# The mLSTM gates' vector steps spread among the input projections, and two output-gate stores issued by ScalarE, in a hybrid encoder layer

## The chip, the cores and the metric

The kernel runs on one core of one Trainium2 chip. The core has five engines with a queue of their own: TensorE (PE in the profile; its weight loads are PEld), VectorE (DVE), ScalarE (ACT), GpSimd (POOL) and SyncE (SP), which here only issues DMA transfers. The engines run side by side and wait for each other through semaphores; each engine takes its own instructions in the order in which they were written to its queue. The metric is the device time of one execution, in microseconds (us).

## The reference

One encoder layer for 2048 tokens of width 1024. A normalised and modulated input goes through one combined projection whose columns feed two groups of heads: windowed attention, and a bidirectional chunkwise mLSTM with 4 heads of 128. Both are normalised, joined, projected and added; then comes a SwiGLU feed-forward part.

```python
proj = hmix @ w_in
q_a, k_a, v_a, q_m, k_m, v_m, o_m, gates = jnp.split(proj, IN_SPLITS, axis=-1)
att = banded_attention(q_a, k_a, v_a, sink)
qk = jax.nn.silu(centred_dwconv(jnp.concatenate([q_m, k_m], axis=-1), conv_w, conv_b))
i_f, f_f, i_b, f_b = jnp.split(gates + b_gates, 4, axis=-1)
h_fwd = mlstm_chunkwise(qm, km, vm, i_f, f_f)
h_bwd = flip(mlstm_chunkwise(flip(qm), flip(km), flip(vm), flip(i_b), flip(f_b)))
h_m = sigmoid(o_m) * rms_norm(h_fwd + h_bwd)
x = x + gate1 * (jnp.concatenate([att, h_m], axis=-1) @ w_out)
```

What the change touches is, first, the gates of the mLSTM. Per direction, head and chunk of 128 tokens:

```python
logf = blocks(jax.nn.log_sigmoid(f_pre))
bcum = jnp.cumsum(logf, axis=-1)
a = b_last[..., None] - bcum + ig
w = jnp.exp(a - jnp.max(a, axis=-1)[..., None])
m_new = jnp.maximum(bl + m_st, am)            # over the chunks, in order
decay = jnp.exp(bl + m_st - m_new)
m_t = jnp.maximum(bcum + m_prev, running maximum)
inter = jnp.exp(g - m_t)
```

There are 2 directions x 4 heads x 16 chunks = 128 rows of 128 tokens, so that all gates fit in one 128 x 128 tile. Second, it touches the store of the output gate o_m (a tanh of it, kept in DRAM until the heads are joined).

## The kernel before

**Stages.** Tokens are handled in NB = 4 blocks of 512 and NT = 16 chunks of 128. The core normalises and transposes the input (hT), multiplies the natural-order columns (values and gate pre-activations, gn), then runs the transposed projections with the convolution (`conv_tile`), the mLSTM, attention with further projections in between, the output projection, and the feed-forward part.

**A projection.** `proj_mm` (L497) writes 24 matmuls of 128x512 for one block (8 parts of the contraction, each with three products of split operands) into a PSUM buffer gps, of which there are two; so the third block can begin only when the first block's buffer has been read for the last time. `conv_tile` does the four blocks of one head's q or k. When a block's matmuls are written, ACT evicts it with the middle tap (cacc, L524) and two edge columns (L525); DVE later reads the same PSUM buffer twice for the other two taps (`sides`, L511 and L512), which frees it. ACT then takes a tanh (ctanh), DVE one more step on it (L121, from the helper `beat`), and SP stores the block (qk_d).

**The order.** In this part the order of DVE, ACT, POOL and SP is the order of the program text (`manual_schedule`), and PE's is that of the matmuls in the text too. A loop of 252 steps sets it: at step i it first lets the generators whose due step has come write their next piece, and then `pull(1)` writes one projection matmul and counts down the list `soon`, in which `sides` and the rest were put with a distance in steps:

```python
for i in range(2 * 96 + 60):
    for j, g in enumerate(steps):
        while due[j] <= i:
            due[j] = next(g)
    ...
    pull(1)
```

So a number of a step fixes only the place in each queue: a DVE instruction written at step 52 runs as soon as DVE has done those ahead of it and its inputs are there, and not when PE comes to its 52nd matmul. For a matmul of the gates it is the place among the projection matmuls.

**The generators.** `steps` holds `gates()` and `w_out_ops()`. The second prepares the output projection's weights: SP loads pieces (bx, by), POOL multiplies and subtracts them (L949, L951, four times L962), SP stores them (wo_d). `gates()` is the gate computation. Its text yields the step at which the next piece is due: 2, 52, 60, 68, 92. Its pieces are, in order: the two PE transposes of gn; reductions of the identity that make selection tiles (pick, spot, rowm); the copies out of PSUM, log-sigmoid (Exp, Ln, reciprocal), two scans for the cumulative sum b, r = ig - b, two scans for the running maximum cm, and the last column of each chunk (st); a small matmul rps that turns st by head; a scan over chunks (mn) and its shifted forms (rw); Exp; rx and two small matmuls cps that spread them again; the row values (mc, ux, it, em, wr); four stores to bc_d and three PE transposes into rT, wT and eT.

**Attention.** Outside the stretches ordered by hand a scheduler orders the engines' instructions. Within attention, units of 128 queries x 4 heads go through `score` (PE L780/L781, DVE L784, ACT L786), `normalize` (POOL L800), `transpose` (PE L807; ACT L140 and DVE L141 split the result into apth and aptl) and `values` (PE L819/L820), and `pull` sets projection matmuls between. `o_tiles` makes the output gates: ACT takes a tanh (oth, L569, one buffer), and SP stores it to og_d (L570). There are 16 such stores: four of head 0, written before attention begins, and then those of head 1 and of heads 2 and 3.

Of the kernel before, what the change touches and what calls it, by code (L numbers as in the profile page):

```python
# [17 lines left out]
MUL, ADD, SUB, MAX, MIN = ALU.mult, ALU.add, ALU.subtract, ALU.max, ALU.min  # L18
# [7 lines left out]
NT = T // P  # L26
# [10 lines left out]
def hybrid_layer_kernel(  # L37
# [5 lines left out]
    pe, dve, act, pool, sp = nc.tensor, nc.vector, nc.scalar, nc.gpsimd, nc.sync  # L43
    x, out = x[0], out[0]
# [513 lines left out]
    def o_tiles(heads, blocks, ws_):  # L558

        if not ws_:  # L560
            ws_.extend(proj_cols(C_OM + h * P) for h in heads)
        for n in blocks:
            for h, w in zip(heads, ws_):
                ps = bank("g", "gps")
                yield from proj_mm(ps, w, n)
                pl, tag = oslots[0]
                oslots.rotate(-1)
                t = pl.tile([P, 512], F32, tag=tag, name="oth", bufs=1)
                act.activation(t, ps, AF.Tanh, scale=0.5)  # L569
                sp.dma_start(og_d[n, :, :, h], t.rearrange("p (c t) -> p c t", c=4))  # L570
# [265 lines left out]
    def gates():  # L836
# [9 lines left out]
        dve.tensor_reduce(out=pick, in_=ident.rearrange("p (q c) -> p q c", c=NT), axis=mybir.AxisListType.X, op=ADD)  # L846
        for sl, o in ((lo_, spot[lo_]), (hi_, spot[hi_, ::-1])):
            dve.tensor_reduce(out=o, in_=ident[sl].rearrange("p (q c) -> p c q", c=NT), axis=mybir.AxisListType.X, op=ADD)
        dve.tensor_copy(rowm, ident[:8, :8].unsqueeze(2).to_broadcast([8, 8, NT]))
# [9 lines left out]
        dve.memset(rw, 0.0)  # L859
        act.activation(e, e, AF.Exp)  # L860
        dve.tensor_scalar(u, e, 1.0, None, ADD)
        act.activation(l, u, AF.Ln)
        dve.scalar_tensor_tensor(t2, u, -1.0, e, ADD, SUB)
        dve.reciprocal(u, u)
        dve.tensor_tensor(t2, t2, u, MUL)
# [3 lines left out]
        dve.tensor_tensor_scan(b[hi_, ::-1], ones[hi_, ::-1], l[hi_, ::-1], 0.0, MUL, ADD)  # L869
        dve.tensor_tensor(r, ig, b, SUB)  # L870
# [6 lines left out]
        yield 52  # L877
# [9 lines left out]
        yield 60  # L887
        act.activation(rw[:, 2], rw[:, 2], AF.Exp)
        yield 68
# [13 lines left out]
        dve.tensor_scalar(ux, cm, mc[:, 0:1], None, MAX)  # L903
        act.activation(it, ux, AF.Exp, bias=mc[:, 0:1], scale=-1.0)
        act.activation(wr, r, AF.Exp, bias=mc[:, 1:2])
        dve.tensor_tensor(em, b, ux, ADD)
        act.activation(em, em, AF.Exp, scale=-1.0)
        dve.tensor_scalar(it, it, float(128 ** -0.5), None, MUL)
        dve.tensor_scalar(ux, ux, -1.0, None, MUL)
        yield 92  # L910
# [1090 lines left out]
```

## Time and profile before

| | |
|---|---|
| median of three runs | 2270.06 us (2265.61 to 2271.12) |
| profiled execution, its own time | 2264.91 us |
| its span | 2263.1 us |
| mean granted clock of TensorE | 0.994 |
| PE busy | 2218.3 us, 98% |
| DVE busy | 1603.8 us, 71% |
| ACT busy | 1060.8 us, 47% |
| POOL busy | 1041.1 us, 46% |
| chain that ended last | PE 88%, DVE 6%, ACT 3%, DMA 2% |

The profile is of one execution. A row of a timeline gives the start in us from the span's beginning, the duration, engine, line, operation, what is written from what, shapes and count; in brackets stands how long the engine idled before it and which instruction's end released it. Several alike are joined in one row (x3). A row of the stretches gives for each engine the busy time, the number of instructions and then PEclk, the clock that TensorE was granted as a share of full speed, the DMA share and GB/s. Idle time of an engine other than the one that sets the pace costs nothing by itself.

### The profile page before, as it was taken

The page shows a single profiled execution, that of the slowest core. Times are in us where ns is not written, and L with a number is a line of the kernel's source. Part 1 is how long each engine was busy: PE and PEld are TensorE (multiplying, and loading weights), DVE is VectorE, ACT ScalarE, POOL GpSimd, SP SyncE. Part 2 cuts the span into 40 slices and gives each one's busy share as a digit, 9 for nine tenths or more (in the row PEclk, how much of TensorE's full clock was granted, in tenths as well). Part 3 has the DMA queues.
Part 4 walks back from the last instruction along what each step waited for, and adds up shares of the span by engine and source line. Part 5 has one row for each costly group of instructions (what it writes and reads, how often), then busy time and mean ns, then how long its engine had stood idle before and what let it go on. Part 6 is the DMA issues. An engine that isn't in the chain of part 4 may idle for free.

```text
span 2263.1 us, 32366 instructions
## 1 busy us (share of the span) xinstructions
PE 2218.3 (98%) x10818; PEld 1858.4 (82%) x10818; DVE 1603.8 (71%) x2942; ACT 1060.8 (47%) x2209; POOL 1041.1 (46%) x904
## 2 busy tenths in 40 slices
PE   6998999999999999999999999999999999999998
PEld 4997888888788878888888888888888888888887
DVE  6775677656688887886667777777767665785694
ACT  5433666544578846354445444433333333233452
POOL 1015635334343333436666664467666664692020
PEclk9999999999999999999999999999999999999999
DMA  8565755685666575764343454534333374543462
GB/s 328 166 204 181 239 170 170 188 241 171 201 188 186 174 248 205 266 236 152 107 147 112 158 181 166 174 126 140 98 112 98 112 259 140 172 149 94 146 216 93
DMA packets 337064, 391.28 MB, mean 173 GB/s; under 512 B 20875, under 2 KB 234235, under 8 KB 336897
## 3 DMA queue, kind: packets, MB, share of 16 engines
q1 hardware_dynamic: 336672, 389.17, 52.7%
q8 instruction: 85, 1.39, 0.3%
q14 instruction: 83, 0.67, 0.1%
q10 hardware_dynamic: 224, 0.04, 0.0%
HBM read 269.95 MB, written 119.19 MB: 172 GB/s over the span
## 4 chain that ended last, share of the span: by engine, by line
PE 88%; DVE 6%; ACT 3%; DMA 2%; issue 1%; POOL 0%; SPq 0%; ACTq 0%; POOLq 0%; DVEq 0%
PE gps L497 14%; PE fp L56 12%; PE fp L57 12%; PE fp L58 12%; PE fo L58 5%; PE fo L57 5%; PE fo L56 5%; PE ops L56 2%; PE ops L58 2%; PE ops L57 2%; PE kvp L621 1%; PE num L708 1%; PE atp L807 1%; PE num L710 1%; PE pv L56 1%
## 5 line engine op out<-in xcount | busy, mean ns | idle before, releaser
L497 PE MATMUL gps<-hT,whi 128*128 128x512 f32 x1088 | 396.5, 419 | 6.8 <-DVE cacc L512 6.8
L58 PE MATMUL fo<-w,al 128*128 128x512 f32 x616 | 239.8, 389 | 0.2 <-DVE al L1755 0.2
L57 PE MATMUL fo<-w,ah 128*128 128x512 f32 x616 | 239.7, 389 | 0.0
L56 PE MATMUL fo<-w,ah 128*128 128x512 f32 x616 | 239.7, 389 | 0.0
L497 PE MATMUL gps<-hT,wlo 128*128 128x512 f32 x544 | 226.6, 417 | 0.0
L497 PEld LDWEIGHTS gps<-hT,whi 128*128 128x128 f32 x1088 | 200.2, 190 | 31.0 <-ACT cacc L528 7.2
L56 PE MATMUL fp<-T,S 128*128 128x512 f32 x528 | 206.7, 391 | 0.1
L57 PE MATMUL fp<-T,S 128*128 128x512 f32 x528 | 205.6, 389 | 0.0
L58 PE MATMUL fp<-T,S 128*128 128x512 f32 x528 | 205.4, 389 | 0.0
L1755 DVE TENSOR_TENSOR al<-al,ah 128x1024 fp32r<-128x1024 f32 x77 | 115.9, 1509 | 106.2 <-ACT ah L1754 106.2
L1754 ACT ACTIVATE ah<-al 128x1024 fp32r<-128x1024 f32 x77 | 81.6, 1060 | 180.4 <-DMA al<-a_d 178.7
L1457 DVE TENSOR_TENSOR S<-sf,S 128x512 fp32r<-128x512 f32 x86 | 127.7, 1523 | 36.8 <-ACT S L1456 36.8
L1457 DVE TENSOR_TENSOR A<-graw,A 128x512 fp32r<-128x512 f32 x86 | 126.4, 1488 | 19.2 <-ACT A L1456 18.9
L58 PE MATMUL fp<-B,A 128*128 128x512 f32 x352 | 136.9, 389 | 0.0
L56 PE MATMUL fp<-B,A 128*128 128x512 f32 x352 | 136.9, 389 | 0.0
L57 PE MATMUL fp<-B,A 128*128 128x512 f32 x352 | 136.9, 389 | 0.0
L58 PEld LDWEIGHTS fo<-w,al 128*128 128x128 f32 x616 | 115.6, 188 | 24.6 <-DVE al L1755 0.6
L56 PEld LDWEIGHTS fo<-w,ah 128*128 128x128 f32 x616 | 115.6, 188 | 24.3
L57 PEld LDWEIGHTS fo<-w,ah 128*128 128x128 f32 x616 | 115.6, 188 | 24.0
L800 POOL TENSOR_SCALAR ap<-ap,adn 128x384 f32<-128x384 f32 (+1 forms) x124 | 70.6, 589 | 133.1 <-PE atp L807 62.0
L1461 POOL TENSOR_TENSOR sf<-A,A22r 128x512 f32<-128x512 f32 x42 | 58.4, 1391 | 150.8 <-DMA A22r<-in_w_ffn_in_dram 133.9
L1624 DVE SCALAR_TENSOR_TENSOR g<-t,g 128x512 f32<-128x512 f32 x44 | 40.9, 929 | 117.6 <-ACT t L1623 117.6
(440 smaller groups left out, 6146.6 us busy)
## 6 DMA issues: line engine op xcount, KB each, us to landing
al<-a_d SPq DMA_DIRECT2D x77, 512.0 KB, 4.2
wmod<-in_w_mod_dram SPq DMA_DIRECT2D x48, 512.0 KB, 7.5
graw<-in_w_ffn_in_dram SPq DMA_DIRECT2D x43, 512.0 KB, 3.9
a_d<-ka SPq DMA_DIRECT2D x66, 256.0 KB, 5.0
bc<-bc_d SPq DMA_DIRECT2D x64, 256.0 KB, 4.4
hop_d<-n SPq DMA_DIRECT2D x56, 256.0 KB, 3.8
a_d<-u SPq DMA_DIRECT2D x55, 256.0 KB, 4.7
mqk<-qk_d SPq DMA_DIRECT2D x44, 256.0 KB, 4.4
```

The source lines that it names most:

```text
L56: pe.matmul(o, lh, rh, start=first, stop=False, skip_group_check=skip)
L57: pe.matmul(o, lh, rl, start=False, stop=False, skip_group_check=skip)
L58: pe.matmul(o, ll, rh, start=False, stop=last, skip_group_check=skip)
L497: pe.matmul(ps, w[i == 2][:, k, :], hT[n](i == 1, k), start=(k == 0 and i == 0), stop=(k == KT - 1 and i == 2))
L621: pe.matmul(kvp[:, :129], kn, vw, start=True, stop=True)
L708: pe.matmul(num[:, d, :129], sc[:, d, :], va_c, start=True, stop=st is None)
L800: pool.tensor_scalar(p, p, dn[:, g:g + 1], 0.0, MUL, ADD)
L1457: dve.tensor_tensor(t[:, 1, :], f, t[:, 0, :].bitcast(F32), SUB)
L1461: add.tensor_tensor(f1, a21, a22, ADD)
L1624: dve.scalar_tensor_tensor(g0, t0, 1.0, g0, ADD, MUL)
L1754: act.activation(ah, al.bitcast(F32), AF.Copy)
L1755: dve.tensor_tensor(al, al.bitcast(F32), ah.bitcast(F32), SUB)
```

## The change

Two edits.

The gate computation keeps its instructions, but its text yields more often: the steps are now 2, 7, 11, 14, 28, 36, 52, 62, 76, 84, 92, 100 and 112. The reductions to pick, spot and rowm move from the front to behind the two scans that make b. The matmul rps moves from step 52 to 62, the matmuls cps from 68 to 84, the stores to bc_d and the final transposes from 92 to 112.

And of the four output-gate stores of head 1, the first two are issued by ACT's queue instead of SP's.

```diff
--- before.py
+++ after.py
@@ -567,7 +567,7 @@
                 oslots.rotate(-1)
                 t = pl.tile([P, 512], F32, tag=tag, name="oth", bufs=1)
                 act.activation(t, ps, AF.Tanh, scale=0.5)
-                sp.dma_start(og_d[n, :, :, h], t.rearrange("p (c t) -> p c t", c=4))
+                (act if heads == (1,) and n < 2 else sp).dma_start(og_d[n, :, :, h], t.rearrange("p (c t) -> p c t", c=4))
 
     later = []
 
@@ -843,10 +843,6 @@
         pick = s2.tile([P, 8], F32, name="pick", bufs=1)
         spot = s2.tile([P, NT], F32, name="spot", bufs=1)
         rowm = s2.tile([8, 8, NT], F32, name="rowm", bufs=1)
-        dve.tensor_reduce(out=pick, in_=ident.rearrange("p (q c) -> p q c", c=NT), axis=mybir.AxisListType.X, op=ADD)
-        for sl, o in ((lo_, spot[lo_]), (hi_, spot[hi_, ::-1])):
-            dve.tensor_reduce(out=o, in_=ident[sl].rearrange("p (q c) -> p c q", c=NT), axis=mybir.AxisListType.X, op=ADD)
-        dve.tensor_copy(rowm, ident[:8, :8].unsqueeze(2).to_broadcast([8, 8, NT]))
         yield 2
         ig, fg = gt("ig"), gt("fg")
         act.activation(fg, ps[:, P:2 * P], AF.Copy)
@@ -857,16 +853,26 @@
         dve.memset(zr, 0.0)
         rw = s2.tile([8, 3, NT], F32, name="rw", bufs=1)
         dve.memset(rw, 0.0)
+        yield 7
         act.activation(e, e, AF.Exp)
+        yield 11
         dve.tensor_scalar(u, e, 1.0, None, ADD)
+        yield 14
         act.activation(l, u, AF.Ln)
         dve.scalar_tensor_tensor(t2, u, -1.0, e, ADD, SUB)
         dve.reciprocal(u, u)
+        yield 28
         dve.tensor_tensor(t2, t2, u, MUL)
         dve.tensor_tensor(l, t2, l, SUB)
         dve.scalar_tensor_tensor(l, fg, 0.0, l, MIN, ADD)
         dve.tensor_tensor_scan(b[lo_], ones[lo_], l[lo_], 0.0, MUL, ADD)
         dve.tensor_tensor_scan(b[hi_, ::-1], ones[hi_, ::-1], l[hi_, ::-1], 0.0, MUL, ADD)
+        yield 36
+        dve.tensor_reduce(out=pick, in_=ident.rearrange("p (q c) -> p q c", c=NT), axis=mybir.AxisListType.X, op=ADD)
+        for sl, o in ((lo_, spot[lo_]), (hi_, spot[hi_, ::-1])):
+            dve.tensor_reduce(out=o, in_=ident[sl].rearrange("p (q c) -> p c q", c=NT), axis=mybir.AxisListType.X, op=ADD)
+        dve.tensor_copy(rowm, ident[:8, :8].unsqueeze(2).to_broadcast([8, 8, NT]))
+        yield 52
         dve.tensor_tensor(r, ig, b, SUB)
         dve.tensor_tensor_scan(cm[lo_], zr[lo_], r[lo_], -3e38, ADD, MAX)
         dve.tensor_tensor_scan(cm[hi_, ::-1], zr[hi_, ::-1], r[hi_, ::-1], -3e38, ADD, MAX)
@@ -874,7 +880,7 @@
         for sl, j in ((lo_, 127), (hi_, 0)):
             dve.tensor_scalar(st[sl, 0], spot[sl], b[sl, j:j + 1], None, MUL)
             dve.scalar_tensor_tensor(st[sl, 1], spot[sl], cm[sl, j:j + 1], st[sl, 0], MUL, ADD)
-        yield 52
+        yield 62
         ps = bank("c", "rps")
         pe.matmul(ps[:8, :2 * NT], pick, st.rearrange("p j c -> p (j c)"), start=True, stop=True)
         sr = s2.tile([8, 2, NT], F32, name="sr", bufs=1)
@@ -884,9 +890,9 @@
         dve.tensor_copy(rw[:, 0, 1:], mn[:, :-1])
         dve.tensor_tensor(rw[:, 1], sr[:, 0], mn, SUB)
         dve.tensor_tensor(rw[:, 2], rw[:, 1], rw[:, 0], ADD)
-        yield 60
+        yield 76
         act.activation(rw[:, 2], rw[:, 2], AF.Exp)
-        yield 68
+        yield 84
         rx = s2.tile([8, 8, NT], F32, name="rx", bufs=1)
         dve.tensor_tensor(rx, rowm, rw[:, 2].unsqueeze(1).to_broadcast([8, 8, NT]), MUL)
         ps = bank("c", "cps")
@@ -901,13 +907,15 @@
         act.activation(q4(dec[:, 64:])[:, :, ::-1], q4(ps[:, P + 64:2 * P]), AF.Copy)
         ux, it, em, wr = gt("gux"), gt("git"), gt("gem"), gt("gwr")
         dve.tensor_scalar(ux, cm, mc[:, 0:1], None, MAX)
+        yield 92
         act.activation(it, ux, AF.Exp, bias=mc[:, 0:1], scale=-1.0)
         act.activation(wr, r, AF.Exp, bias=mc[:, 1:2])
         dve.tensor_tensor(em, b, ux, ADD)
+        yield 100
         act.activation(em, em, AF.Exp, scale=-1.0)
         dve.tensor_scalar(it, it, float(128 ** -0.5), None, MUL)
         dve.tensor_scalar(ux, ux, -1.0, None, MUL)
-        yield 92
+        yield 112
         for d, sl in ((0, lo_), (1, hi_)):
             sp.dma_start(bc_d[:, :, d, :].rearrange("h c t -> (h c) t"), ux[sl])
             sp.dma_start(bc_d[:, :, 2 + d, :].rearrange("h c t -> (h c) t"), it[sl])
```

How the instructions stand. VectorE, at the two scans for b (which the order names SCALAR_TENSOR_TENSOR on L868 and L869 and the profile TENSOR_TENSOR_SCAN); "gates" is the tile of all gate values. Before:

```order
L868 SCALAR_TENSOR_TENSOR gates<-ones_r,gates 64x128
L869 SCALAR_TENSOR_TENSOR gates<-ones_r,gates 64x128
L870 TENSOR_TENSOR gates<-gates 128x128
L871 SCALAR_TENSOR_TENSOR gates<-gates 64x128
L872 SCALAR_TENSOR_TENSOR gates<-gates 64x128
L875 TENSOR_SCALAR st<-spot,gates 64x16
L876 SCALAR_TENSOR_TENSOR st<-spot,gates,st 64x16
L875 TENSOR_SCALAR st<-spot,gates 64x16
L876 SCALAR_TENSOR_TENSOR st<-spot,gates,st 64x16
L511 SCALAR_TENSOR_TENSOR cacc<-gps,cvw,cacc 128x511
L512 SCALAR_TENSOR_TENSOR cacc<-gps,cvw,cacc 128x511
L881 COPY sr<-rps 8x32
```

The same place in the changed kernel (the lines of the new text):

```order
L868 SCALAR_TENSOR_TENSOR gates<-ones_r,gates 64x128
L869 SCALAR_TENSOR_TENSOR gates<-ones_r,gates 64x128
L511 SCALAR_TENSOR_TENSOR cacc<-gps,cvw,cacc 128x511
L512 SCALAR_TENSOR_TENSOR cacc<-gps,cvw,cacc 128x511
L871 TENSOR_REDUCE pick<-ident 128x8
L873 TENSOR_REDUCE spot<-ident 64x16 x2
L874 COPY rowm<-ident 8x128
L876 TENSOR_TENSOR gates<-gates 128x128
L877 SCALAR_TENSOR_TENSOR gates<-gates 64x128
L878 SCALAR_TENSOR_TENSOR gates<-gates 64x128
L881 TENSOR_SCALAR st<-spot,gates 64x16
L882 SCALAR_TENSOR_TENSOR st<-spot,gates,st 64x16
```

L511 and L512 of the first block now stand right behind the scans for b; the reductions and the steps from r to st follow them.

TensorE, at rps, one piece of the difference (gps is the projection's PSUM buffer):

```order
 L497 MATMUL gps<-hT_767,wlo 128x512
 L497 MATMUL gps<-hT_767,whi 128x512
-L879 MATMUL rps<-st,pick 8x32
 L497 MATMUL gps<-hT_771,whi 128x512
 L497 MATMUL gps<-hT_767,wlo 128x512
```

It stands ten projection matmuls further on. In the same way cps goes 16 matmuls further on and the transposes 20.

VectorE, from st to rx, before which PE's cps can't run. Before:

```order
L881 COPY sr<-rps 8x32
L883 SCALAR_TENSOR_TENSOR mn<-sr 8x16
L884 COPY rw<-mn 8x15
L885 TENSOR_TENSOR rw<-sr,mn 8x16
L886 TENSOR_TENSOR rw<-rw 8x16
L511 SCALAR_TENSOR_TENSOR cacc<-gps,cvw,cacc 128x511
L512 SCALAR_TENSOR_TENSOR cacc<-gps,cvw,cacc 128x511
L121 SCALAR_TENSOR_TENSOR cacc<-ctanh,cacc 128x512
L891 TENSOR_TENSOR rx<-rowm,rw 8x128
```

Now:

```order
L511 SCALAR_TENSOR_TENSOR cacc<-gps,cvw,cacc 128x511
L512 SCALAR_TENSOR_TENSOR cacc<-gps,cvw,cacc 128x511
L121 SCALAR_TENSOR_TENSOR cacc<-ctanh,cacc 128x512
L887 COPY sr<-rps 8x32
L889 SCALAR_TENSOR_TENSOR mn<-sr 8x16
L890 COPY rw<-mn 8x15
L891 TENSOR_TENSOR rw<-sr,mn 8x16
L892 TENSOR_TENSOR rw<-rw 8x16
L511 SCALAR_TENSOR_TENSOR cacc<-gps,cvw,cacc 128x511
L512 SCALAR_TENSOR_TENSOR cacc<-gps,cvw,cacc 128x511
L897 TENSOR_TENSOR rx<-rowm,rw 8x128
```

The convolution's steps of one more block (L511, L512 of block 1 and L121 of block 0) stand ahead of sr, and those of block 2 ahead of rx.

ScalarE, at the first of the two moved stores, one piece of the difference:

```order
 L569 ACTIVATE oth<-gps 128x512
 L792 ACTIVATE adn<-adn 128x4
-L140 ACTIVATE apth<-atp 128x512 x3
+L140 ACTIVATE apth<-atp 128x512
+L570 DMA og_d<-oth 512x1x128
+L140 ACTIVATE apth<-atp 128x512 x2
 L786 ACTIVATE ap,ars<-ap,nmx 128x256 x3
```

The store stands behind the first of three apth copies; the second store follows its tanh directly. In VectorE's queue the scheduler sets one L784 of the next unit ahead of the second and third aptl at this place. All else in attention and behind it stands as before.

## The prediction

> **What bounds the kernel now.** I read the page's first lines and its costliest groups, then the waits of PE, PE's timeline with the granted clock by stretch and the chain of waits around the longest wait, and at last the timelines of DVE, ACT and POOL there.
>
> ```profile
> span 2263.1 us, 32366 instructions
> PE 2218.3 (98%) x10818; PEld 1858.4 (82%) x10818; DVE 1603.8 (71%) x2942; ACT 1060.8 (47%) x2209; POOL 1041.1 (46%) x904
> L497 PE MATMUL gps<-hT,whi 128*128 128x512 f32 x1088 | 396.5, 419 | 6.8 <-DVE cacc L512 6.8
> ```
>
> PE is busy for 98% of the span: what an edit is worth is what it takes from, or adds to, PE's idle time and cold clock. The projections' matmuls (L497) wait for 6.8 us in all, in one piece, on DVE's L512. Timeline of PE, one piece of the chain of waits (matmuls at full pace), and stretches (busy time of PE, PEld, DVE, ACT and POOL, then PEclk):
>
> ```profile
> 192.69 1.19 PE L497 MATMUL gps<-hT,whi 128*128 128x512 f32 x2 [6.83 <-DVE cacc L512]
> 194.66 0.28 PE L879 MATMUL rps<-st,pick 128*8 128x32 f32 x2
> ...
> 199.81 0.46 PE L894 MATMUL cps<-rx,ones_r 8*128 8x128 f32 x2
> 200.20 0.50 PE L497 MATMUL gps<-hT,wlo 128*128 128x512 f32 x1
> ...
> 206.27 36.31 PE gps L497 x160
> ...
> 185.90:192.60 6.70, 0.00 (x0) 0.00 (x0) 6.46 (x8) 1.50 (x4) 6.54 (x9) 0.80 0.55 181
> 192.70:196.70 4.00, 4.00 (x10) 2.71 (x11) 1.62 (x5) 1.83 (x2) 4.00 (x5) 0.50 0.00 0
> ```
>
> PE stops at 185.86 (192.69 less 6.83), when block 2 of the first tile wants the PSUM buffer of block 0. After it the clock is 0.50 for 4.0 us, which costs 2.0 us more. So 8.8 us is all that the gate part can give back. At full pace a matmul takes 36.31/160 = 0.227 us.
>
> Why L512 is late (DVE, then POOL, then one row of ACT):
>
> ```profile
> 176.70 0.28 DVE L846 TENSOR_REDUCE pick<-ident 128x8 f32<-128x128 f32 x1
> ...
> 177.79 0.27 DVE L855 SCALAR_TENSOR_TENSOR gates<-gates 128x128 f32<-128x128 f32 x1
> ...
> 182.03 1.55 DVE L868 TENSOR_TENSOR_SCAN gates<-ones_r,gates 64x128 f32<-64x128 f32 x1
> 183.59 1.36 DVE L869 TENSOR_TENSOR_SCAN gates<-ones_r,gates 64x128 f32<-64x128 f32 x1
> 184.99 0.65 DVE L870 TENSOR_TENSOR gates<-gates 128x128 f32<-128x128 f32 x1
> 185.67 0.83 DVE L871 TENSOR_TENSOR_SCAN gates<-gates 64x128 f32<-64x128 f32 x1
> ...
> 187.88 1.19 DVE L876 SCALAR_TENSOR_TENSOR st<-spot,gates,st 64x16 f32<-64x16 f32 x1
> 189.08 1.21 DVE L875 TENSOR_SCALAR st<-spot,gates 64x16 f32<-64x16 f32 x1
> 190.33 0.65 DVE L876 SCALAR_TENSOR_TENSOR st<-spot,gates,st 64x16 f32<-64x16 f32 x1
> 191.01 0.75 DVE L511 SCALAR_TENSOR_TENSOR cacc<-gps,cvw,cacc 128x511 f32<-128x511 f32 x1
> 191.79 0.75 DVE L512 SCALAR_TENSOR_TENSOR cacc<-gps,cvw,cacc 128x511 f32<-128x511 f32 x1
> 194.98 0.18 DVE L881 COPY sr<-rps 8x32 f32<-8x32 f32 x1 [2.44 <-PE rps L879]
> ...
> 196.40 0.60 DVE L886 TENSOR_TENSOR rw<-rw 8x16 f32<-8x16 f32 x1
> ...
> 198.42 0.68 DVE L121 SCALAR_TENSOR_TENSOR cacc<-ctanh,cacc 128x512 f32<-128x512 f32 x1
> 199.02 0.27 DVE L891 TENSOR_TENSOR rx<-rowm,rw 8x128 f32<-8x128 f32 x1
> ```
>
> ```profile
> 182.02 1.28 POOL L949 TENSOR_TENSOR bx<-bx,gb 128x512 f32<-128x512 f32 x1 [18.18 <-DMA gb<-gate_d]
> 183.26 1.41 POOL L951 TENSOR_TENSOR by<-by,gb 128x512 f32<-128x512 f32 x1
> ...
> 185.44 0.78 POOL L962 TENSOR_TENSOR ts<-by,bx 128x256 f32<-128x256 f32 x1
> ...
> 187.78 1.26 POOL L949 TENSOR_TENSOR bx<-bx,gb 128x512 f32<-128x512 f32 x1
> 189.00 1.26 POOL L951 TENSOR_TENSOR by<-by,gb 128x512 f32<-128x512 f32 x1
> 190.22 0.72 POOL L962 TENSOR_TENSOR ts<-bx 128x256 f32<-128x256 f32 x1
> ...
> 191.58 1.53 POOL L962 TENSOR_TENSOR ts<-by,ts 128x256 f32<-128x256 f32 x2
> ...
> 196.92 1.56 POOL L962 TENSOR_TENSOR ts<-by,ts 128x256 f32<-128x256 f32 x2
> ```
>
> ```profile
> 181.13 0.16 ACT L525 ACTIVATE edge<-gps 128x2 f32<-128x2 f32 x1
> ```
>
> L511 stands behind the whole gate chain, though its input was ready at 181.29. And that chain is slow for another reason than its work: from 182.02 to 198.48 POOL runs without a gap, and DVE's small steps end just when a POOL instruction ends. L876 ends at 189.07, POOL's L949 at 189.04; the next L875 at 190.29, POOL's L951 at 190.26; the next L876 at 190.98, POOL's L962 at 190.94. L871 ends 0.28 after POOL's 186.22. While POOL runs, such a step costs one POOL instruction, whatever its size. L511 and L512, with one operand in PSUM, take 0.75 beside POOL all the same.
>
> **The change, part by part.**
>
> The late reductions. pick, spot and rowm leave the front: from 176.70 to 177.79 is 1.09 us, so everything to the first scan moves 1.09 earlier (the new steps at 7, 11, 14 and 28 change no order on DVE there). L868 starts at 180.94, before POOL's first instruction; free, a scan needs 0.28 (L871 after its release), and with the next one's gap b is done near 181.7 instead of 184.95. The gain here is 3.2, of which two POOL waits are 2.3.
>
> L511 and L512 of block 0 then come right behind: 181.7 to 183.2 (1.53 for the pair, 191.01 to 192.54). PE wants the buffer at 185.86. The wait of 6.83 goes, and the 2.0 of cold clock with it: -8.8, with 2.6 us to spare. What is late next are the three places where PE itself waits for the gates; their matmuls stood after 52, 68 and 92 projection matmuls and now after 62, 84 and 112.
>
> rps (after 62). DVE does the reductions from 183.2; their own 1.09 gives 184.3, as the bound from below. The seven steps r, cm, cm and st four times (L870 to the last L876, two of them left out above) took 184.99 to 190.98 before, 6.0 us, and meet the same POOL instructions now: r ends with the one that ends near 184.7, the last with L951 at 190.26. So st is done near 190.3. PE comes to rps 14 matmuls after 185.8, at 189.0: a new wait of 1.4 us. No row shows a reduction beside POOL. If each of the four also waited for a POOL instruction, st would come four later, near 193.1, and the wait be 4.2. I take the lower bound: a reduction reads one operand from SBUF, as L511 does, and L511 is not held in these rows.
> [...]
>
> cps (after 84). Behind st stand L511 and L512 of block 1 (to 191.8), L121 of block 0 (two SBUF operands: from the end of the first of the two L962 at 191.58, near 192.35, to 193.0, by its 0.68), then sr to the second rw. These five took 194.98 to 197.00, 2.0 us; here two of the POOL instructions that they meet are of the long kind (1.26 for 0.75), so 2.0 to 3.3, and I take the upper: 196.3. L511 and L512 of block 2 follow (197.85), and rx, in 0.27, or 0.9 behind a POOL end: 198.7. Before, rx ended at 199.29 and the projections went on at 200.20, 0.91 later, of which the two cps are most; now at 199.6. But PE has then done 84 matmuls and not 68. Before it had done 84 at 200.20 + 16 x 0.227 = 203.8. Gain: 4.2 us. That number holds whatever PE lost at rps, since DVE's chain sets it: PE reaches cps at 190.6 + 22 x 0.227 = 195.6 and waits some 3 us. So of 8.8 us some 4.6 come back as two new waits.
>
> The transposes (after 112). PE is there at 199.6 + 28 x 0.227 = 206. The last Exp needs block 3's eviction on ACT, which is in front of it in the new order (block ends at 202.3, four ACT rows of some 1.6 us in all): near 204.3. Free by 1.7; without that cover each us late is a us of PE. The split Exps cost nothing else: no activation table is loaded more often than before, by the order.
>
> Queues. SP has the four bc_d stores later, behind two groups of wo_d stores and one weight load; the first mLSTM load of bc comes after 252 projection matmuls, some 30 us later. POOL's order is the same. qk_d's first store waits for L121, now 5 us earlier, so SP's loads for POOL's fourth group move earlier and not later. Zero.
>
> Attention. Two og_d stores go from SP to ACT:
>
> ```profile
> 681.27 0.60 ACT L569 ACTIVATE oth<-gps 128x512 f32<-128x512 f32 x1
> 681.86 1.56 ACT L140 ACTIVATE apth<-atp 128x512 fp32r<-128x512 f32 x3
> ...
> 682.20 0.57 SPq L570 DMA_DIRECT2D og_d<-oth  x1
> ...
> 695.85 0.62 ACT L786 ACTIVATE ap<-ap,nmx 128x384 f32<-128x384 f32 x1 [0.91 <-DVE nmx L784]
> ```
>
> An issue holds SP's queue for 0.57; ACT's row for it does not exist, so I use that. The first one stands behind one apth, with two apth and the next exponentials queued: at most 0.57 later, at least 0, since ACT is still busy with the first apth while its queue issues. DVE's order answers with one L784 ahead of the second aptl. The second store stands ahead of an L786 that idles for 0.91 anyway: free. The gain on SP is nothing, as PE waits for none of these loads there. From -0.2 to +0.6; I take 0.
>
> Sum: -8.8 + 4.6 + 0 = -4.2 us. The profiled execution took 2264.91 (span 2263.1 and 1.8 around it) and would take 2260.7. It is 5.15 below the median of the three runs, 2270.06, and below all of them. I set the change against the median: 2265.9 us.
>
> **The rivals.**
>
> More is hidden. If the steps behind the reductions are held only half as long, rps is free and rx ends 3 us earlier: a gain of 7 to 8.8, 2261.3 to 2263. For it: the whole chain holds only about 4 us of work of its own. Against it: of the steps that stay beside POOL four are shown above to end within 0.04 of a POOL instruction.
>
> The new idle cools the clock, or the reductions are held too.
>
> ```profile
> 582.00:598.00 16.00, 12.21 (x63) 9.46 (x61) 8.46 (x32) 9.52 (x29) 3.22 (x6) 1.00 0.67 203
> 826.00:837.00 11.00, 6.22 (x21) 4.54 (x20) 7.97 (x12) 6.01 (x10) 8.01 (x7) 0.75 0.14 48
> ```
>
> With 3.8 of 16 us idle in pieces the clock stayed at 1.00; with 4.8 of 11 idle it fell to half for half the time. The new place has 1.4 + 3.1 idle in some 10.7, between the two. Half clock for up to 3.4 us costs up to 1.7; all four reductions held moves rx by 2.8. Gain 0 to 2.7: 2267.4 to 2270.
> [...]
>
> Slower: the gates' chain becomes the bound. PE now has to pass rps, cps and the transposes in its own order. From the point at which rx ends later than 203.8 - 0.91 = 202.9, the change loses, 1 us for each us. My rx is at 198.7, 201.5 with the reductions held; if all later steps met 1.26 us instructions of POOL as well, near 204: 2271, and over 0.3% only with a second such delay at the transposes. An ACT queue held by its stores is no such case: 0.6 us.
>
> **How the numbers follow.** 0.3%, 6.8 us, is about what a measurement of this kernel can tell from no change. The forecast (gain 3 to 5.5) has 0.52, more hidden 0.20, cold clock or held reductions 0.20, slower 0.08. Over 6.8 us faster are half of the second case and a tenth of the first, with the runs' spread of 5.5 us: 0.19. Slower by over 0.3% is most of the last: 0.06; the same 0.75. The range reaches from the gain of 8.8, less a little for spread, to the slower rival's 2271: 2259.5 to 2271.0.
>
> **What would show it.** Right: no wait of L497 on L512; L868 under 0.5 us; PE's rps waits 1 to 2 us for st and cps 2 to 4 us for rx; the 84th projection matmul about 4 us earlier; two og_d issues on ACT's queue with no new wait of PE near 682. Wrong: rps waiting over 3 us, a clock of 0.5 after either wait, a wait at the transposes, or the attention stretch longer by over 1 us.

## The result, and the profile after

The changed kernel takes 2263.01 us (median of nine runs, 2257.91 to 2264.89) against 2267.03 us for the kernel before, run beside it (nine runs, 2265.61 to 2271.12): ratio 0.9977, 95% interval 0.9967 to 0.9987. That is 4.0 us or 0.23% less, inside the 0.3% that the prediction called no change. The profiled execution took 2262.92 us.

First lines and the projections' group of the page after:

```profile
span 2261.1 us, 32357 instructions
PE 2219.7 (98%) x10818; PEld 1858.9 (82%) x10818; DVE 1611.6 (71%) x2942; ACT 1061.4 (47%) x2209; POOL 1041.5 (46%) x904
L497 PE MATMUL gps<-hT,whi 128*128 128x512 f32 x1088 | 395.1, 418 | 0.0
```

The 6.8 us of waiting on L512 have left the projections' group. PE's timeline after shows what came instead; behind it two stretches, whose column behind POOL's is the granted clock:

```profile
191.52 0.23 PE L885 MATMUL rps<-st,pick 128*8 128x32 f32 x2 [1.66 <-DVE st L882]
196.93 0.40 PE L899 MATMUL cps<-rw,rowm 8*128 8x32 f32 x2
199.41 0.48 PE L900 MATMUL cps<-rx,ones_r 8*128 8x128 f32 x2 [2.08 <-DVE rx L897]
206.31 0.49 PE L924 MATMUL gps<-ident,gates 128*128 128x128 f32 x3
```

```profile
185.00:195.00 10.00, 8.34 (x38) 6.53 (x37) 9.63 (x15) 4.11 (x8) 9.84 (x12) 1.00 0.46 146
195.00:206.00 11.00, 8.92 (x40) 7.04 (x39) 10.18 (x17) 4.81 (x16) 10.81 (x12) 1.00 0.67 213
```

Two waits, on st and on rx, and none at the transposes (L924); the clock stayed full here. DVE and POOL after:

```profile
181.78 0.42 DVE L868 TENSOR_TENSOR_SCAN gates<-ones_r,gates 64x128 f32<-64x128 f32 x1
182.21 0.42 DVE L869 TENSOR_TENSOR_SCAN gates<-ones_r,gates 64x128 f32<-64x128 f32 x1
...
183.45 0.75 DVE L512 SCALAR_TENSOR_TENSOR cacc<-gps,cvw,cacc 128x511 f32<-128x511 f32 x1
184.11 0.28 DVE L871 TENSOR_REDUCE pick<-ident 128x8 f32<-128x128 f32 x1
184.31 0.76 DVE L873 TENSOR_REDUCE spot<-ident 64x16 f32<-64x128 f32 x2
185.07 0.64 DVE L874 COPY rowm<-ident 8x128 f32<-8x128 f32 x1
...
189.01 1.23 DVE L881 TENSOR_SCALAR st<-spot,gates 64x16 f32<-64x16 f32 x1
190.28 1.19 DVE L882 SCALAR_TENSOR_TENSOR st<-spot,gates,st 64x16 f32<-64x16 f32 x1
...
198.62 0.73 DVE L897 TENSOR_TENSOR rx<-rowm,rw 8x128 f32<-8x128 f32 x1
```

```profile
183.09 1.29 POOL L957 TENSOR_TENSOR bx<-bx,gb 128x512 f32<-128x512 f32 x1 [18.76 <-DMA gb<-gate_d]
...
188.93 1.28 POOL L957 TENSOR_TENSOR bx<-bx,gb 128x512 f32<-128x512 f32 x1
190.17 1.27 POOL L959 TENSOR_TENSOR by<-by,gb 128x512 f32<-128x512 f32 x1
```

The scans run ahead of POOL and take 0.42 us each (1.55 and 1.36 before). The steps of st still end with POOL's instructions: L881 at 190.24 and POOL's L957 at 190.21, the last L882 at 191.47 and L959 at 191.44.

To follow the gain through the kernel I use the evictions of the projections' blocks (ACT L524) as clock marks. First and fifth block before, then after:

```profile
180.46 0.78 ACT L524 ACTIVATE cacc<-gps,cvb,cvw 128x512 f32<-128x512 f32 x1 [0.42 <-PE gps L497]
...
212.70 0.78 ACT L524 ACTIVATE cacc<-gps,cvb,cvw 128x512 f32<-128x512 f32 x1 [2.31 <-PE gps L497]
```

```profile
181.28 0.78 ACT L524 ACTIVATE cacc<-gps,cvb,cvw 128x512 f32<-128x512 f32 x1 [1.50 <-PE gps L497]
...
208.69 0.78 ACT L524 ACTIVATE cacc<-gps,cvb,cvw 128x512 f32<-128x512 f32 x1 [1.28 <-PE gps L497]
```

I call the time between the two "the gate stretch": 32.24 us before, 27.41 after, a gain of 4.83. This execution came to the stretch 0.82 us later, so on the profile's own scale the kernel is 4.0 us ahead at the fifth block. At 333 us it gives 1.5 us back, and at about 590 us it regains 1.1. By the evictions of the feed-forward part it gives back 1.2 more between 813 and 997 us and 0.7 by 1462 us. So the two profiled executions end only 2.0 us apart (2264.91 and 2262.92), where the medians differ by 4.0.

The two stores, ScalarE's rows and its queue:

```profile
678.16 0.59 ACT L140 ACTIVATE apth<-atp 128x512 fp32r<-128x512 f32 x1
678.20 0.59 ACTq L570 DMA_DIRECT2D og_d<-oth  x1
...
691.18 0.52 ACTq L570 DMA_DIRECT2D og_d<-oth  x1
```

Their issues take 0.59 and 0.52 us on ACT's queue, beside ACT's own work, and the next apth begins some 0.2 us later than it would back to back (678.84); PE's waits from 650 to 720 us are the same as before (0.4 us on aptl).

### The profile page after: what moved, and what is told of

It reads as the page before. It is cut to its first block, busy times and chain, and to the rows that moved or that the text cites. A ratio compares the mean times of both kernels' runs of the same rounds, so it can differ in the third digit from the quotient of the medians.

```text
span 2261.1 us, 32357 instructions
## 1 busy us (share of the span) xinstructions
PE 2219.7 (98%) x10818; PEld 1858.9 (82%) x10818; DVE 1611.6 (71%) x2942; ACT 1061.4 (47%) x2209; POOL 1041.5 (46%) x904
## 4 chain that ended last, share of the span: by engine, by line
PE 88%; DVE 5%; ACT 2%; DMA 2%; issue 1%; POOL 1%; SPq 0%; POOLq 0%; ACTq 0%; DVEq 0%
PE gps L497 15%; PE fp L56 12%; PE fp L57 12%; PE fp L58 12%; PE fo L58 5%; PE fo L57 5%; PE fo L56 5%; PE ops L56 2%; PE ops L58 2%; PE ops L57 2%; PE atp L807 1%; PE num L708 1%; PE kvp L621 1%; PE num L710 1%; PE pv L56 1%
```

## The experiments

The theory, from the prediction: POOL's instructions hold DVE's small steps one for one; the wait on L512 goes because L511 and L512 no longer stand behind the steps of st; and the chain, still held by POOL, comes back as waits at rps and cps. The rivals: the chain's own length or order makes the waits, the reductions' place is what counts, the cooled clock eats the gain, or the stores matter. The table at the end gives for each kernel the gate stretch, and how much longer it is than in the run in which PE waits for nothing there.

**The two edits apart.** The gates' new order with all stores on SP:

```diff
-(act if heads == (1,) and n < 2 else sp).dma_start(og_d[n, :, :, h], ...)
+sp.dma_start(og_d[n, :, :, h], ...)
```

> The gate part of the change alone; all og_d stores stay on SP. Theory (the gate part carries all of it): as the whole change, some 4 to 5 us below the kernel before (ratio 0.998), the same two PE waits, about 1.7 us at rps and 2.1 us at cps, and no wait of L497 on L512. Rival (the two stores bring a part): at least 1 us less gain than the whole change, and PE idle longer around the two stores in attention.

Measured: 2262.66 us, ratio 0.9981 (0.9972 to 0.9990). And the kernel before with the two stores on ACT alone:

> The kernel before with only the two og_d stores moved to ACT's queue. Theory: within 0.6 us of the kernel before (ratio 0.9997 to 1.0003), the wait of 6.8 us on L512 unchanged. Rival: 1 us or more below (SP was in the way) or above (ACT's issue of 0.55 us holds the apth copies and PE waits for them).

Measured: 2267.18 us beside 2267.41, ratio 0.9998 (0.9990 to 1.0007). The stores change nothing that these runs can tell (the interval reaches from 2.3 us below to 1.6 above), so the gates' order carries the gain. In the traces the stores are worth some 0.1 us, between 680 and 686 us: the nine kernels that have them gain it there against the kernel before, and the two others don't. The expectation of an unchanged wait on L512 missed: it was 0.9 us longer, though DVE's order there is the same. POOL's first instruction came 0.90 us behind the first block's eviction here, against 1.56 in the kernel before, and so held L866 and L867 as well (1.41 and 1.26 us against 0.29 each):

```profile
194.41 1.19 PE L497 MATMUL gps<-hT,whi 128*128 128x512 f32 x2 [7.71 <-DVE cacc L512]
```

What the clock did with the gates alone was unexpected. Its two waits, 1.57 and 1.74 us, are no longer than those of the changed kernel, yet here the clock fell (1.00 in both stretches there):

```profile
185.00:200.00 15.00, 11.69 (x50) 8.96 (x49) 13.66 (x24) 5.69 (x13) 14.34 (x17) 0.96 0.63 199
200.00:215.00 15.00, 15.00 (x64) 12.22 (x63) 9.73 (x14) 5.65 (x14) 8.85 (x10) 0.92 0.74 231
```

**POOL taken away from the kernel before.** Its products and differences for the first four pieces of w_out are left out:

```diff
-            pool.tensor_tensor(bx, bx, gb[c_], MUL)
+            if n > 3:
+                pool.tensor_tensor(bx, bx, gb[c_], MUL)
...
-            for t, f, g in (...):
-                pool.tensor_tensor(t, f, g, SUB)
+            if n > 3:
+                for t, f, g in (...):
+                    pool.tensor_tensor(t, f, g, SUB)
```

> The kernel before, with POOL's products and differences for the first four of eight pieces of w_out left out (the pieces are stored as they were loaded), so that POOL is idle during the gate chain; DVE's order is that of before. Theory (DVE's small steps are held by POOL's instructions): the scans take about 0.4 us each instead of 1.55 and 1.36, the four st steps together under 1 us instead of 3.6, PE's wait on L512 falls from 6.8 us to about 0.7, the clock stays at 1.00: some 7.5 us below the kernel before (ratio 0.9967), with no step of the gates moved. Rival (the steps are slow by themselves): the wait stays above 5 us and the time within 2 us of the kernel before.

Measured: 2262.58 us, ratio 0.9976 (0.9967 to 0.9985). DVE and PE, with no work moved at all:

```profile
182.50 0.42 DVE L868 TENSOR_TENSOR_SCAN gates<-ones_r,gates 64x128 f32<-64x128 f32 x1
...
184.58 0.23 DVE L875 TENSOR_SCALAR st<-spot,gates 64x16 f32<-64x16 f32 x1
```

```profile
187.30 0.70 PE L497 MATMUL gps<-hT,whi 128*128 128x512 f32 x2 [0.97 <-ACT edge L525]
```

The scans fall from 1.55 to 0.42 us, a step of st from up to 1.21 to 0.23, and the wait of 6.83 us to 0.97. (The row names ACT's edge column, which ended last, at 187.20; L512 ended at 187.15, as far ahead of PE as in the kernel before.) The gate stretch gains 7.6 us, as expected. The total gains only 4.8 of the 7.5: from 237 to 255 us and at 333 us some of it is given back (2.2 and 0.75 us by the evictions).

**The same taken from the changed kernel.**

> The changed kernel without GpSimd's products and differences for the first four pieces of w_out (so the weights of those pieces, and the output, differ); GpSimd has nothing to do until about 200 us. If GpSimd's instructions are what holds VectorE's small steps, the four st steps take 0.23 us each as in the kernel before without that work, st ends at about 187.5 us, the wait for rps is gone and that for cps is 0.3 us or less; the gain by the fifth block is 7.5 to 8.8 us and the kernel some 3.5 us below the changed one (2 us if part is given back at the mLSTM of the next heads, as in the kernel before without that work). If the waits come from the chain's own length, they stay at 1 to 2 us each and the time is that of the changed kernel within 1 us.

Measured: 2257.52 us, ratio 0.9962 (0.9950 to 0.9975), 5.6 us below the changed kernel beside it, where 2 to 3.5 were expected. PE has no wait between 175 and 232 us; the steps of st:

```profile
186.81 0.24 DVE L881 TENSOR_SCALAR st<-spot,gates 64x16 f32<-64x16 f32 x1
187.08 0.23 DVE L882 SCALAR_TENSOR_TENSOR st<-spot,gates,st 64x16 f32<-64x16 f32 x1
```

With POOL's work gone both new waits are gone, so they are POOL's doing and not the chain's own length. The gate stretch is 23.38 us, the gain 8.86: all of the 8.8 us that the prediction said could be had.

**The changed kernel again.**

> The changed kernel once more, as the measure for the three beside it and as a second profiled execution. By the theory the two new waits of TensorE stand where they stood, on st L882 for the rps matmul and on rx L897 for the cps matmul, 1.5 to 2.1 us each, and the projections' fifth block is 4 to 5 us earlier against its start than in the kernel before. Open is the clock behind the two waits: 1.00 in one profile (1.66 and 2.08 us of waiting), 0.92 to 0.96 in the profile of the gates' move alone (1.6 and 1.7 us). If the waits cool it by chance of the moment, it may be either here, and the gain then differs by some 1 us between executions.

Measured: 2263.12 us, ratio 0.9984 (0.9975 to 0.9993). The waits were 1.57 and 1.77 us, and this time the clock fell. The two waits and three stretches of this run:

```profile
191.76 0.23 PE L885 MATMUL rps<-st,pick 128*8 128x32 f32 x2 [1.57 <-DVE st L882]
...
199.31 0.48 PE L900 MATMUL cps<-rx,ones_r 8*128 8x128 f32 x2 [1.77 <-DVE rx L897]
```

```profile
197.50:199.30 1.80, 0.04 (x1) 0.00 (x0) 1.65 (x4) 0.73 (x2) 1.72 (x4) 1.00 1.00 297
...
200.00:201.00 1.00, 1.00 (x3) 0.70 (x3) 1.00 (x7) 0.80 (x4) 0.61 (x1) 0.50 0.49 166
...
203.00:204.00 1.00, 1.00 (x5) 0.77 (x5) 1.00 (x2) 0.00 (x0) 1.00 (x2) 0.82 0.96 246
```

Half clock from about 200.0 to 203.4 us costs half of 3.4, some 1.7 us. The gate stretch gained 3.64 us here and 4.83 in the other execution.

**The reductions back at the front**, everything else as changed:

```diff
+        dve.tensor_reduce(out=pick, ...)
+        ...
+        dve.tensor_copy(rowm, ...)
         yield 2
...
-        yield 36
-        dve.tensor_reduce(out=pick, ...)
-        ...
-        dve.tensor_copy(rowm, ...)
         yield 52
```

> The changed kernel with the three reductions and the copy to rowm back ahead of the gates' first steps, where they stood before. The prediction's theory has two parts for them: 1.09 us leave the front, and through it the scans L868 and L869 run before GpSimd's first instruction. If the second part holds, the scans start about 1 us later, run into GpSimd's start at 183.1 us and take 0.8 to 1.2 us each instead of 0.42; L512 of the first block ends at 185 to 186.5 us against 185.86, when TensorE wants its buffer, so a wait of up to 1 us on L512 may come back; the reductions are then out of the way of st, so that the wait for rps stays at 1.5 to 3 us. The whole: 0 to 1.5 us above the changed kernel. The rival: the place of the two convolution steps right behind the scans is all that matters, and the scans stay at 0.42 us: then no wait on L512, st ends 1 to 1.5 us earlier, the wait for rps shrinks to 0.5 us and the kernel is 1 us below the changed one.

Measured: 2262.31 us, ratio 0.9978 (0.9969 to 0.9987); the changed kernel beside it 0.9984 (0.9975 to 0.9993).

```profile
182.17 1.52 DVE L872 TENSOR_TENSOR_SCAN gates<-ones_r,gates 64x128 f32<-64x128 f32 x1
183.70 1.35 DVE L873 TENSOR_TENSOR_SCAN gates<-ones_r,gates 64x128 f32<-64x128 f32 x1
```

```profile
186.76 0.70 PE L497 MATMUL gps<-hT,whi 128*128 128x512 f32 x2 [0.78 <-DVE cacc L512]
192.63 0.23 PE L884 MATMUL rps<-st,pick 128*8 128x32 f32 x2 [2.42 <-DVE st L881]
199.62 0.40 PE L898 MATMUL cps<-rw,rowm 8*128 8x32 f32 x2
```

The steps went the way that the theory said, though not all by its sizes: the scans meet POOL again (and take 1.52 and 1.35 us, longer than the 0.8 to 1.2 expected), 0.78 us of the wait on L512 comes back, and rps waits longer. But the time is not 0 to 1.5 us above the changed kernel, it is 0.8 below, within the intervals. For cps waits no more: PE comes to it later, by 1.63 us of longer waits and by half clock from 194.2 to 197.6 us, ahead of cps here, which costs 1.7. The waits are 3.20 us in sum against 3.34 in the changed kernel beside it, and the gate stretch is 28.54 against 28.60. Here, where on DVE's chain the time is lost decides only which matmul waits. That L512's wait is 0.78 here and not 6.83 shows that the place of L511 and L512 gives 6.0 of it, and the move of the reductions 0.8.

**The gates' matmuls later on PE.** The waits at rps and cps could be met by more projection matmuls ahead of them:

```diff
-        yield 62
+        yield 76
         ps = bank("c", "rps")
...
+        yield 82
         sr = ...
...
-        yield 76
+        yield 104
         act.activation(rw[:, 2], rw[:, 2], AF.Exp)
-        yield 84
+        yield 106
         rx = ...
+        yield 120
         ps = bank("c", "cps")
```

and 92, 100, 112 become 128, 134, 148.

> The changed kernel with the gates' matmuls later on PE: rps after 76 projection matmuls instead of 62, cps after 120 instead of 84, the transposes after 148 instead of 112, and sr to the second rw behind L511 and L512 of block 2. Theory (the two waits are only a matter of where PE meets the chain): both waits vanish, 3.7 us below the changed kernel, about 8 us below the kernel before (ratio 0.9963 to 0.997). Rival (the DVE chain beside POOL is too slow for PE wherever they meet): a wait of 2 us or more turns up at a projection's PSUM buffer or at the transposes, and the time stays within 1 us of the changed kernel.

Measured: 2260.67 us, ratio 0.9973 (0.9963 to 0.9983); gate stretch 24.69. The waits at rps and cps vanish, but the time is 2.4 us below the changed kernel and 6.7 below the kernel before, not 3.7 and 8. One wait has come in their place, half of what the rival asked for, on the second block's L512, which stands behind st:

```profile
192.35 0.73 PE L497 MATMUL gps<-hT,whi 128*128 128x512 f32 x2 [1.03 <-DVE cacc L512]
```

**The steps of st behind the second block too** (52 becomes 60, 76 becomes 88, and the rest 4 to 10 later):

> The run with later matmuls of the gates, with the steps from r to st put behind the two convolution steps of the second block too (count 60 instead of 52), and the matmul of rps at 88, the steps behind it at 92, 108, 110, 124, 132, 138 and 152. By the theory the last wait there, 1.03 us on L512 of the second block, goes as well, no wait of the gates is left on TensorE, the gain by the fifth block is 8.0 to 8.8 us (7.55 before this edit), and the time is 0.5 to 1.2 us below the run with later matmuls, if it is kept to the end. The rival: the steps of st now fall into the third block, and L512 of the third or fourth block is late in its turn: a wait of 1 us or more on L512 stays, only at another block, and the time is the same within 0.5 us.

Measured: 2261.02 us, ratio 0.9972 (0.9961 to 0.9982). The rival was right: the wait went from the start of the fourth block (on L512 of the second) to the start of the fifth (on L512 of the third), 0.95 us, just under the 1 us that it named.

```profile
199.36 0.73 PE L497 MATMUL gps<-hT,whi 128*128 128x512 f32 x2 [0.95 <-DVE cacc L512]
```

The fifth block's eviction is 8.85 us better, but only because the matmuls of cps and the transposes stand behind it in this kernel. By the ninth block, which comes behind all of them in every kernel, the gain is 7.62 us, against 7.55 in the run before it; and the total is that of the run before it.

**The reductions where DVE is idle.** DVE waits 1.07 us for ScalarE's Ln ahead of the reciprocal (L863 after). The reductions and rowm go there, in the changed kernel and in the run with later matmuls:

```diff
         dve.scalar_tensor_tensor(t2, u, -1.0, e, ADD, SUB)
+        dve.tensor_reduce(out=pick, ...)
+        ...
+        dve.tensor_copy(rowm, ...)
         dve.reciprocal(u, u)
...
-        yield 36
-        dve.tensor_reduce(out=pick, ...)
-        ...
-        dve.tensor_copy(rowm, ...)
```

> The changed kernel with the three reductions and the copy to rowm neither at the front nor beside GpSimd, but in the 1.07 us in which VectorE waits for ScalarE's Ln (ahead of the reciprocal); all else as changed. By the theory they are free there: the scans stay at 0.42 us each, and r starts where pick started, 1.5 us earlier (184.1 instead of 185.6 us). The seven steps from r to st still end with GpSimd's instructions, so that st ends 1.3 to 2.4 us earlier; the wait for rps falls from 1.7 to 0.4 us or less, that for cps from 2.1 to 1 us or less, and the gain by the fifth block rises from 3.6 to 4.8 us to 7 to 8.8 us; the kernel is some 3 us below the changed one, 2260 us. The rival: the steps only meet other, longer GpSimd instructions, st ends less than 0.6 us earlier, and the two waits keep 2.5 us or more in sum; then the time is that of the changed kernel within 1 us.

Measured: 2261.78 us beside 2267.51, ratio 0.9977 (0.9968 to 0.9986).

```profile
190.20 0.22 PE L884 MATMUL rps<-st,pick 128*8 128x32 f32 x2 [0.29 <-DVE st L881]
195.59 0.40 PE L898 MATMUL cps<-rw,rowm 8*128 8x32 f32 x2
197.37 0.48 PE L899 MATMUL cps<-rx,ones_r 8*128 8x128 f32 x2 [1.38 <-DVE rx L896]
```

The waits fall from 3.3 to 3.7 us to 1.67, the clock stays at 1.00, the gate stretch gains 6.89, just short of the 7 to 8.8 expected; cps kept more than the 1 us allowed. At 333 us 1.9 and at 590 us, against the kernel before, another 1.9 were given back. The total is 1.2 us below the changed kernel's and not 3, less than its interval.

> The run with later matmuls of the gates, with the reductions and rowm in the wait for Ln as well. By the theory L512 of the second block ends 1.3 to 1.6 us earlier than there (192.2 us), against the 1.03 us that TensorE still waited for it, so no wait of TensorE on the gates is left between 175 and 230 us, the clock stays at 1.00, and the gain by the fifth block is 8.4 to 8.9 us (7.55 without this edit). The time is 0.5 to 1.2 us below the run with later matmuls if the gain is kept. The rival: the later stretches give it back, as the stretch at 333 us did with up to 1.8 us, and the time is the same within 0.5 us.

Measured: 2258.29 us, ratio 0.9962 (0.9949 to 0.9974): 9.2 us below the kernel before and the best here with the whole work done, some 4.7 below the changed kernel (the two intervals overlap a little). The gate stretch gained 8.04, not 8.4 to 8.9. The median lies 2.4 us below that of the run with later matmuls, though the gate stretch is only 0.5 shorter; at 333 us this run gives back 0.9 and that one 1.8, and the rest is within the intervals. The wait on the second block's L512 only halved:

```profile
192.87 0.74 PE L497 MATMUL gps<-hT,whi 128*128 128x512 f32 x2 [0.50 <-DVE cacc L512]
```

because r started 0.22 us behind the start of a POOL instruction and ended 0.15 behind its end. DVE and POOL in this run:

```profile
184.35 1.24 DVE L875 TENSOR_TENSOR gates<-gates 128x128 f32<-128x128 f32 x1
```

```profile
184.13 1.31 POOL L960 TENSOR_TENSOR by<-by,gb 128x512 f32<-128x512 f32 x1
```

In the run above it started 0.26 us ahead of the end of the POOL instruction then running, ended 0.15 behind it too, and so took 0.41 us:

```profile
184.16 0.41 DVE L875 TENSOR_TENSOR gates<-gates 128x128 f32<-128x128 f32 x1
```

```profile
183.13 1.29 POOL L956 TENSOR_TENSOR bx<-bx,gb 128x512 f32<-128x512 f32 x1 [18.40 <-DMA gb<-gate_d]
```

**All kernels together.** Waits are PE's in the gate stretch; the clock is that of 185 to 200 and 200 to 215 us; "lost" is the gate stretch over the 23.38 us of the run without waits. In the row of st behind the second block the stretch leaves out cps and the transposes, so "lost" is taken there at the ninth block; in the other rows the ninth block gives what the fifth gives.

| kernel | waits, us | clock | gate stretch | lost | median |
|---|---|---|---|---|---|
| before | 6.83 | 0.77, 1.00 | 32.24 | 8.86 | 2267.03 |
| stores only | 7.71 | 0.66, 1.00 | 33.82 | 10.44 | 2267.18 |
| changed | 3.74 | 1.00, 1.00 | 27.41 | 4.03 | 2263.01 |
| changed, again | 3.34 | 1.00, 0.89 | 28.60 | 5.22 | 2263.12 |
| gates only | 3.31 | 0.96, 0.92 | 28.53 | 5.15 | 2262.66 |
| reductions at the front | 3.20 | 0.89, 1.00 | 28.54 | 5.16 | 2262.31 |
| reductions in Ln's wait | 1.67 | 1.00, 1.00 | 25.35 | 1.97 | 2261.78 |
| later matmuls | 1.03 | 1.00, 1.00 | 24.69 | 1.31 | 2260.67 |
| both | 0.50 | 1.00, 1.00 | 24.20 | 0.82 | 2258.29 |
| st behind the second block | 0.95 | 1.00, 1.00 | 23.39 | 1.24 | 2261.02 |
| before, without POOL | 0.97 | 1.00, 1.00 | 24.62 | 1.24 | 2262.58 |
| changed, without POOL | 0 | 1.00, 1.00 | 23.38 | 0 | 2257.52 |

With the full clock, "lost" is the waits, where there are any, plus 0.3 us; where it fell, the waits plus 1.8 to 2.7. The medians follow less closely: they belong to three groups of runs, each beside its own kernel before (2267.41, 2266.92, 2267.51), and what later stretches give back differs.

## Why the prediction was right

**The number.** The forecast was a gain of 4.2 us; the medians say 4.0. The 2265.9 us lie 2.9 above the 2263.01 measured, because the three runs shown had the high median of 2270.06 and nine runs of the same kernel 2267.03. By that alone the time stands at the edge of the band that the rival with more hidden named (2261.3 to 2263), while its gain of 7 to 8.8 did not come. The gate stretch gained 4.83 and 3.64 us in two executions of the changed kernel, the forecast's 4.2 between them. That the total came so near to 4.2 is in part luck: some terms below were off in opposite directions, and later stretches moved the gain by 1 to 2 us, which the forecast did not have.

**-8.8, the wait on L512 and its cold clock: right.** Taking off the 0.82 us by which the execution came later, the scans began at 180.96 (forecast 180.94), took 0.42 us each instead of 0.28, and L512 of the first block ended at about 183.4 (183.2). The run without POOL's work gained 8.86: the most that could be had was sized right. The forecast left open how much the departure of the reductions gives. The run with them at the front, against the repeated run, settled it: their departure took 0.78 us from the wait on L512 and 0.85 from that at rps (2.42 to 1.57), and 1.77 came back at cps, where in the run with them at the front the clock had fallen ahead of it.

**rps, 1.4: right, 0.2 to 0.3 short.** Measured 1.57 to 1.66. After the change st ended with the POOL instruction that the forecast named, and that one ended later: at 191.44, on the forecast's scale 190.62, against 190.26. In the repeated run st ended with the one behind it.

One term was too small, the copy to rowm, counted inside the reductions' own 1.09 us: beside POOL it took 0.64 us instead of 0.21. Since the steps behind it end with POOL's instructions, how much of this reached the wait is not shown. The reductions themselves were not held (0.28, and 0.76 for two, against 0.28 and 0.74 before). The forecast argued for all four from the one operand that they read. The rows bear that out for the three reductions and not for the copy, which reads one operand too and ended at 185.71, 0.07 behind POOL's L959; what sets the copy apart is not shown.

**cps, "some 3 us": the size too high.** Measured 2.08, 1.77, 1.74. rx ended at 198.5 by the forecast's scale (forecast 198.7); but the first two cps matmuls, 0.40 us, don't need rx and ran ahead of the wait, and PE came 0.5 us later than 22 matmuls of 0.227 would have it. What counts is the place of the 84th matmul, and it was set by rx as forecast. It came 0.6 us earlier than forecast, at 199.0 instead of 199.6, since PE went on 0.47 us behind the end of rx and not 0.91: this is the difference between the gain of 4.83 and the 4.2.

**The clock: a rival that came true in part.** It was given 0.20, as a case instead of the forecast. In three of four profiled executions with the two waits (or their like) the clock halved for some 3.4 us, which costs 1.7 us, the very size given; in one it didn't. Its gain was put at 0 to 2.7, and it measured 3.6 to 3.7, since without the drop the gain is 4.8 and not 4.2, the two waits were 0.4 us shorter in sum than in the execution at full clock, and the reductions were not held. The 3.4 us of that case stand in no row that the forecast shows; the profile before has one stretch at half clock of that length, from 49.9 to 53.3 us, beside longer ones (6.8 us, from 189.9 to 196.7).

What sets off a drop is not shown. By the granted clock each lasted some 3.4 us: 200.0 to 203.4 in the repeated run, 198.9 to 202.3 with the gates alone, 194.2 to 197.6 with the reductions at the front. The longest single wait ahead of them was 1.77, 1.74 and 2.42 us; the 2.08 us in the first execution of the changed kernel were followed by none.

**Transposes, queues, attention, each zero: right.** There is no wait at L924, and the stores alone gave 0.9998.

**What the forecast left out.** It took the gain at the fifth block for the gain at the end. At 333 us, where the mLSTM takes its next head, between nothing and 1.9 us is given back. What the profiles show there, without a run that tests it, is that SP's load of mv ahead of an mqk load took long to issue, and that PE waited for mqk and for the step on mv. After, and then the best run:

```profile
328.55 1.45 SPq L583 DMA_DIRECT2D mv<-vaug_d  x1
```

```profile
325.57 0.40 SPq L583 DMA_DIRECT2D mv<-vaug_d  x1
```

PE's waits there after the change (before, no wait of this kind stood there):

```profile
331.84 0.30 PE L611 MATMUL ktp<-ident,mqk 128*128 128x128 f32 x1 [0.35 <-DMA mqk<-qk_d]
...
337.98 0.49 PE L621 MATMUL kvp<-vw,kn 128*128 128x129 f32 x2 [0.69 <-ACT vw L616]
```

In the seven runs where that issue took 1.29 to 1.95 us, 0.7 to 1.9 us were lost there; where it took 0.37 to 0.40 (before and four runs), 0 to 0.85. Why the issue takes longer in some kernels stays open. So do the changes at 590 us and in the feed-forward part, and with them why medians rank a little differently from the gate stretches.

## What to carry to other kernels

When a wait is removed by moving work behind it, follow the same chain to the next place where the bounding engine needs its end: the chain's length doesn't change, and here about half of the gain came back there. Ask next what makes the chain long: the seven steps from r to st took 2.2 us beside an idle GpSimd (185.13 to 187.31 in the changed kernel without POOL's work) and 5.8 beside a busy one (185.64 to 191.47), so steps that read nothing late belong in a stretch where VectorE idles anyway, and the consumers belong later on TensorE. Both together gave about twice the gain of the change (8.04 us in the gate stretch against 4.83 and 3.64; 9.2 by the medians against 4.0).

## What the hardware showed that was not expected

- A 64x16 step takes 0.23 us beside an idle GpSimd and 0.53 to 1.24 beside a busy one. Where in a GpSimd instruction a step starts decides over 0.8 us: r took 0.41 us where it started 0.26 ahead of the end of one, and 1.24 where it started 0.22 behind the start of one. The gate chain can therefore differ by 0.9 us between kernels at places where nothing was changed (wait on L512 6.83 and 7.71).
- Two separate waits of 1.6 to 2.1 us, some 6 us apart, were followed by half clock in two of three profiles, within 0.7 us of the end of the second (1.74 and 1.77 us), and not in the third, where they were the longest.
- A store of 256 KB issued by ScalarE's queue took 0.59 and 0.52 us to issue, and the activations around it ran at their usual durations (apth 0.59), the one behind it some 0.2 us later.
